# Rotary embedding on one core: VectorE at 8 positions a time, and an early 1 MB store between the second and the third load

## The chip, the cores and the metric

The kernel runs on one core of a Trainium2 chip. The metric is device time in microseconds (us) of that core, lower is better. The profile covers a slightly shorter span than the timed execution (316.0 us against 317.6 us for the kernel before). All positions in time below are counted from the start of the profile's span.

## The reference

The input x is float32, (batch 8, sequence 2048, heads 16, head size 64), 67.1 MB. Neighbouring elements of a head form pairs, and every pair is rotated by an angle that depends on the position. The output has the shape and type of x.

```python
x_pairs = x.reshape(batch, seq_len, num_heads, head_dim // 2, 2)
x1, x2 = x_pairs[..., 0], x_pairs[..., 1]
out1 = x1 * cos - x2 * sin
out2 = x1 * sin + x2 * cos
out = np.stack([out1, out2], axis=-1).reshape(batch, seq_len, num_heads, head_dim)
```

There is little arithmetic for each byte. 67.1 MB must be read and 67.1 MB written.

## The kernel before

One batch is one tile of 128 partitions x 16 positions x 1024 elements. GpSimd's DMA queue loads it and casts it from float32 to bf16 on the way (8 MB are read, 4 MB land in SBUF: 67.63 MB read from HBM in all, and 4096 KB listed for a load), and its stores cast back (67.11 MB written). Five tiles are in flight. Loads and stores are numbered by batch, from 0, so load 2 is the third load. VectorE rotates a tile in place, a few positions at a time, with three instructions: the product with the sine table, the product with the cosine table, and a sum that swaps the neighbours.

```python
KP = 4        # positions in one group of VectorE instructions
NX = 5        # tiles in flight
HEAD = 2      # positions of batch 0 that take another way in
TAIL = 4      # positions of batch 7 that take another way out

def load(b, k0=0):
    if b not in tiles:
        tiles[b] = xpool.tile([P, K, HD], bf16, name="xt")
    nc.gpsimd.dma_start(out=tiles[b][:, k0:], in_=x_t[b, :, k0:])

def store(b, k1=K):
    nc.gpsimd.dma_start(out=out_t[b, :, :k1], in_=tiles[b][:, :k1])

def rotate(b, k0, k1):
    # ... views cut ...
    nc.vector.tensor_tensor(out=rows(qt[:, :nk]), in0=rows(xp), in1=tab(s_tab), op=mult)
    nc.vector.tensor_tensor(out=rows(xp), in0=rows(xp), in1=tab(c_tab), op=mult)
    # ...
    nc.vector.tensor_tensor(out=x3, in0=x3, in1=q_swap, op=add)
```

SyncE's DMA queue brings the first two positions of batch 0 in float32 ("head", 2 x 512 KB), then the cosine table and the sine table (256 KB each). Beside it, GpSimd issues all five loads.

```python
head = stage.tile([P, TAIL, HD], fp32, name="st")
for k in range(HEAD):
    nc.sync.dma_start(out=head[:, k : k + 1], in_=x_t[0, :, k : k + 1])
nc.sync.dma_start(out=cos_sb, in_=cos_t)
nc.sync.dma_start(out=sin_sb, in_=sin_t)
load(0, HEAD)
for b in range(1, NX):
    load(b)

nc.scalar.copy(out=tiles[0][:, :HEAD], in_=head[:, :HEAD])
# ... VectorE makes the bf16 tables s_tab and c_tab from sin_sb and cos_sb ...
for b in range(B):
    if b == 0:
        rotate(b, 0, HEAD)
        rotate(b, HEAD, KP)
    for k0 in range(KP if b == 0 else 0, K, KP):
        rotate(b, k0, k0 + KP)
    if b < B - 1:
        store(b)
    if b >= 1 and b - 1 + NX < B:
        load(b - 1 + NX)
# ... the last batch: 12 positions by GpSimd's queue, 4 by ScalarE's cast and SyncE's queue ...
```

## Time and profile before

The time before is 317.61 us (median of 5 runs, 317.44 to 317.65).

| what | kernel before |
|---|---|
| span of the profile | 316.0 us |
| VectorE busy | 221.8 us, 102 instructions |
| GpSimd's DMA queue, share of 16 engines | 96.8% |
| HBM traffic over the span | 134.7 MB, 426 GB/s |
| sine table lands | 44.2 us |
| last store issued by GpSimd | 262.7 us |

First the page's own lines. The row "DMA" gives the busy share of the DMA engines in 40 equal slices, in tenths, and the q lines give packets, megabytes and share of 16 engines:

```profile
span 316.0 us, 198 instructions
...
DVE 221.8 (70%) x102; ACT 6.9 (2%) x4; POOL 8.9 (3%) x20
...
DMA  9899999999999999999999999999999999999996
...
q0 software_dynamic: 2304, 98.04, 96.8%
q1 hardware_dynamic: 720, 3.67, 3.1%
...
HBM read 67.63 MB, written 67.11 MB: 426 GB/s over the span
```

The DMA engines are full from the second slice to the last but one. VectorE is busy 70% of the span, and nearly all of its idle time lies at the two ends. The reading is that the kernel is bound by its DMA queue.

The packet counts are worth a division. GpSimd's queue made 16 transfers and has 2304 packets, SyncE's made 5 and has 720. Both give 144 packets a transfer, or 9 on each of 16 engines, whether a transfer moves 8 MB or 256 KB. The packed trace also holds the start, length and size of every single packet, which no printed view shows. By these records 8 of the 9 carry data and one carries 4 bytes, and a data packet of load 1 lands 32 KB where one of a table lands 2 KB.

The waits (engine, line, what it waited for: total us, number of times, longest):

```profile
ACT xt L116 <- DMA out_dram<-xt: 286.3, 1, 286.3
POOL out_dram L59 <- DVE xt L80: 202.1, 8, 70.5
POOL xt L56 <- DMA out_dram<-xt: 51.3, 3, 21.7
DVE s_tab L94 <- DMA sin_sb<-in_sin_dram: 44.2, 1, 44.2
```

VectorE's only wait for a DMA is the first one: 44.2 us for the sine table (L94 makes the bf16 sine table). Cosine is already there at 24.04 us (issued at 1.64, 22.4 us to landing). The timeline shows what follows (start, duration, engine, line; L56 is the load, L59 the store, L74, L75 and L80 the three rotation instructions, L116 the copy that waits until the store of batch 6 has landed):

```profile
1.24 2.80 POOL L56 DMA_DIRECT2D xt<-in_x_dram  x5 [0.80 <-PEq L144]
...
44.22 0.45 DVE L94 CAST s_tab<-sin_sb 128x512 bf16<-128x512 f32 x1 [44.22 <-DMA sin_sb<-in_sin_dram]
...
45.50 1.22 DVE L74 TENSOR_TENSOR qt<-xt,s_tab 128x2048 bf16<-128x2048 bf16 x1
...
48.02 1.23 DVE L80 TENSOR_TENSOR xt<-xt,qt 128x2048 bf16<-128x2048 bf16 x1
...
74.53 0.54 POOL L59 DMA_DIRECT2D out_dram<-xt  x1 [70.48 <-DVE xt L80]
...
262.71 0.53 POOL L59 DMA_DIRECT2D out_dram<-xt  x1 [20.41 <-DVE xt L80]
...
295.87 0.19 ACT L116 COPY xt<-xt 1x1 bf16<-1x1 bf16 x1 [286.31 <-DMA out_dram<-xt]
```

All five loads are issued within 4 us. The first store is issued at 74.5 us, the last at 262.7, and the DMA engines are busy until 314.8 us.

### The profile page before, as it was taken

The page shows a single profiled execution, that of the slowest core. Times are in us where ns is not written, and L with a number is a line of the kernel's source. Part 1 is how long each engine was busy: PE and PEld are TensorE (multiplying, and loading weights), DVE is VectorE, ACT ScalarE, POOL GpSimd, SP SyncE. Part 2 cuts the span into 40 slices and gives each one's busy share as a digit, 9 for nine tenths or more (in the row PEclk, how much of TensorE's full clock was granted, in tenths as well). Part 3 has the DMA queues.
Part 4 walks back from the last instruction along what each step waited for, and adds up shares of the span by engine and source line. Part 5 has one row for each costly group of instructions (what it writes and reads, how often), then busy time and mean ns, then how long its engine had stood idle before and what let it go on. Part 6 is the DMA issues. An engine that isn't in the chain of part 4 may idle for free.

```text
span 316.0 us, 198 instructions
## 1 busy us (share of the span) xinstructions
DVE 221.8 (70%) x102; ACT 6.9 (2%) x4; POOL 8.9 (3%) x20
## 2 busy tenths in 40 slices
DVE  0000039999999999999999999999999999100000
ACT  1200000000000000000000000000000000000400
POOL 3000000000000000000000000000000000000000
DMA  9899999999999999999999999999999999999996
GB/s 241 198 257 212 212 207 236 228 199 199 253 212 265 398 498 431 398 332 261 203 399 465 328 203 199 481 448 265 199 307 423 398 440 481 406 398 481 417 431 263
DMA packets 3025, 101.72 MB, mean 322 GB/s; under 512 B 336, under 2 KB 336, under 8 KB 848
## 3 DMA queue, kind: packets, MB, share of 16 engines
q0 software_dynamic: 2304, 98.04, 96.8%
q1 hardware_dynamic: 720, 3.67, 3.1%
q14 instruction: 1, 0.01, 0.0%
HBM read 67.63 MB, written 67.11 MB: 426 GB/s over the span
## 4 chain that ended last, share of the span: by engine, by line
another core or an unknown queue 91%; DMA 2%; ACTq 1%; ACT 1%; SPq 0%; issue 0%
DMA st<-in_x_dram 2%; ACTq L144 1%; ACT xt L92 1%; ACT L92 0%; SPq L85 0%; ACT xt L116 0%; ACTq L116 0%; ACTq L92 0%
## 5 line engine op out<-in xcount | busy, mean ns | idle before, releaser
L75 DVE TENSOR_TENSOR xt<-xt,c_tab 128x4096 bf16<-128x4096 bf16 (+1 forms) x33 | 73.5, 2228 | 1.1
L80 DVE TENSOR_TENSOR xt<-xt,qt 128x4096 bf16<-128x4096 bf16 (+1 forms) x33 | 73.5, 2228 | 1.1
L74 DVE TENSOR_TENSOR qt<-xt,s_tab 128x4096 bf16<-128x4096 bf16 (+1 forms) x33 | 73.5, 2228 | 1.1
L94 DVE CAST s_tab<-sin_sb 128x512 bf16<-128x512 f32 x1 | 0.5, 453 | 44.2 <-DMA sin_sb<-in_sin_dram 44.2
L59 POOL DMA_DIRECT2D out_dram<-xt x8 | 4.3, 535 | 202.1 <-DVE xt L80 202.1
L116 ACT COPY xt<-xt 1x1 bf16<-1x1 bf16 x1 | 0.2, 193 | 286.3 <-DMA out_dram<-xt 286.3
L56 POOL DMA_DIRECT2D xt<-in_x_dram x8 | 4.4, 561 | 52.1 <-DMA out_dram<-xt 51.3
L117 ACT CAST st<-xt 128x4096 f32<-128x4096 bf16 x1 | 3.6, 3599 | 0.0
L92 ACT CAST xt<-st 128x2048 bf16<-128x2048 f32 x1 | 1.9, 1899 | 0.0
L92 ACT ACT_TABLE_LOAD x1 | 1.3, 1283 | 6.4 <-DMA st<-in_x_dram 6.4
L96 DVE CAST c_tab<-cos_sb 128x1024 bf16<-128x1024 f32 x1 | 0.7, 684 | 0.0
L95 DVE TENSOR_SCALAR s_tab<-sin_sb 128x512 bf16<-128x512 f32 x1 | 0.4, 443 | 0.0
L133 POOL MEMSET const-float32-0.0<- 128x1 f32 x1 | 0.1, 99 | 0.2 <-issue 0.2
L133 POOL MEMSET const-bfloat16-1.0<- 128x1 bf16 x1 | 0.1, 102 | 0.0
L133 POOL MEMSET const-float32-1.0<- 128x1 f32 x1 | 0.1, 99 | 0.0
L133 POOL MEMSET const-uint8-127<- 128x1 uint8 x1 | 0.1, 99 | 0.0
## 6 DMA issues: line engine op xcount, KB each, us to landing
xt<-in_x_dram POOLq DMA_DIRECT2D x7, 4096.0 KB, 58.0
out_dram<-xt POOLq DMA_DIRECT2D x1, 6144.0 KB, 49.4
xt<-in_x_dram POOLq DMA_DIRECT2D x1, 3584.0 KB, 22.7
out_dram<-st SPq DMA_DIRECT2D x1, 2048.0 KB, 15.5
st<-in_x_dram SPq DMA_DIRECT2D x2, 512.0 KB, 4.5
cos_sb<-in_cos_dram SPq DMA_DIRECT2D x1, 256.0 KB, 22.4
sin_sb<-in_sin_dram SPq DMA_DIRECT2D x1, 256.0 KB, 42.1
out_dram<-xt POOLq DMA_DIRECT2D x7, 54.0
```

Source lines behind the costliest of these rows:

```text
L56: nc.gpsimd.dma_start(out=tiles[b][:, k0:], in_=x_t[b, :, k0:])
L59: nc.gpsimd.dma_start(out=out_t[b, :, :k1], in_=tiles[b][:, :k1])
L74: nc.vector.tensor_tensor(out=rows(qt[:, :nk]), in0=rows(xp), in1=tab(s_tab), op=mult)
L75: nc.vector.tensor_tensor(out=rows(xp), in0=rows(xp), in1=tab(c_tab), op=mult)
L80: nc.vector.tensor_tensor(out=x3, in0=x3, in1=q_swap, op=add)
L92: nc.scalar.copy(out=tiles[0][:, :HEAD], in_=head[:, :HEAD])
L94: nc.vector.tensor_copy(out=s2[:, :, 0], in_=sin_sb)
L95: nc.vector.tensor_scalar_mul(s2[:, :, 1], sin_sb, -1.0)
L96: nc.vector.tensor_copy(out=c_tab.rearrange("p k (i j) -> p (k i) j", j=2), in_=cos_sb.to_broadcast([P, K * D2, 2]),)
L117: nc.scalar.copy(out=tail, in_=tiles[B - 1][:, K - TAIL :])
L133: nc = _bacc.Bacc("TRN2", target_bir_lowering=False, num_devices=1)
L144: with _tile.TileContext(nc) as tc:
```

## The change

It does two things. VectorE works on 8 positions at a time, so 48 instructions (102 before, 54 after) and their fixed costs go (about 159 ns each, an estimate from 1226 ns at 128x2048 and 2293 ns at 128x4096). And GpSimd, having issued two loads, stores the first two rotated positions of batch 0 (1 MB of output) before it issues loads 2 to 4: output should start to flow early. No byte is added.

```diff
-    KP = 4
+    KP = 8
...
-    def store(b, k1=K):
-        nc.gpsimd.dma_start(out=out_t[b, :, :k1], in_=tiles[b][:, :k1])
+    def store(b, k0=0, k1=K):
+        nc.gpsimd.dma_start(out=out_t[b, :, k0:k1], in_=tiles[b][:, k0:k1])
...
         load(0, HEAD)
-        for b in range(1, NX):
-            load(b)
+        load(1)
...
             if b == 0:
                 rotate(b, 0, HEAD)
+                store(b, 0, HEAD)
+                for c in range(2, NX):
+                    load(c)
                 rotate(b, HEAD, KP)
...
-                store(b)
+                store(b, HEAD if b == 0 else 0)
```

More of the change, by code (lines that the diff above doesn't have):

```diff
@@ L106 @@
             if b < B - 1:
-                store(b)
+                store(b, HEAD if b == 0 else 0)
             if b >= 1 and b - 1 + NX < B:
                 load(b - 1 + NX)
-        store(B - 1, K - TAIL)
+        store(B - 1, 0, K - TAIL)
         tail = stage.tile([P, TAIL, HD], fp32, name="st")
```

## The prediction

> **What bounds the kernel now.** The DMA engines. The slices of the page show them 90% busy or more from the second slice to the last but one, and the queue table gives 96.8% to the GpSimd queue and 3.1% to the SyncE queue. HBM moves 134.7 MB in a 316.0 us span (426 GB/s). VectorE is busy 221.8 us (70%) and in the timeline runs without a gap from 44.2 to 269.4 us, yet the last store issue is at 262.7 and the queue drains until about 314.
>
> **VectorE at 8 positions.** Groups by form: 1226 ns at 128x2048, 2293 ns at 128x4096, so about 159 ns is fixed per instruction (estimate) and one of 128x8192 should take about 4427 ns. 50 instructions fewer save about 9 us of VectorE (busy about 213 us). None of it is on the critical path.
>
> **The early store.** No byte is added or removed. But GpSimd issues in order, and the third load now stands behind a store that waits for the first rotation. That rotation needs the sine table. Its 256 KB, issued at 2.1 us, lands only at 44.2 us. Cosine landed at 24.04 us, and load 0 at about 23.9 (1.24 + 22.7). The DMA engines seem to alternate between the two queues packet by packet[...]. Both queues show 144 packets per full transfer (2304/16 and 720/5), so one small table keeps pace with one 8 MB load, and sine lands when load 1 lands. Estimate from bytes: 23.9 + 8.65 MB/425 GB/s = 44.2 us.
>
> In the old kernel load 2 is already queued then. In the new one the queue is empty at about 44 us, and refilling takes the chain:
> - tables, 44.22 to 45.50: 1.3 us
> - first rotation, three 128x2048: 45.50 to 49.25: 3.75 us
> - VectorE to GpSimd, 0.55 us (as before the first old store), and issue, 0.54 us
> - restart and landing latency, [...] here the first 512 KB load took 3.9 us to land, which leaves about 2.7 us (estimate)
>
> Sum: about 8.2 to 8.8 us with idle DMA engines, between about 43 and 51 us. All of it is critical, because everything after it is a queue that is never empty: loads 2 to 4 and the stores follow back to back and merely move about 8 us later. VectorE would wait for loads 6 and 7 (landing about 209 and 248 us, it being ready about 207 and 236), still ahead of the queue, so harmless.
>
> **Predicted:** 317.6 + 8.4 = 326.0 us; 8 in 10: 322.8 to 328.2. Faster by over 2%: 0.02; within 2%: 0.16; slower by over 2%: 0.82.
>
> **What would show it.** In the new profile: DMA near 0 from about 43.5 to 51 us, the rest unchanged at 1.0; sine still landing near 44 us; GpSimd's first store issue near 49.8; VectorE x52, 128x8192 near 4.43 us, its work no longer gapless near the last batch; store 6 landing, which releases the last copy, near 304 instead of 295.8.
>
> **What would make it wrong.** If sine lands well before load 1, the hole shrinks by as much, toward "same". If stores and loads mixed differently run faster than 430 GB/s, part is won back. If the restart takes longer than 2.7 us, it is slower.

The sum came to 8.2 to 8.8 us. The first terms make 6.1 us; the 2.7 us of the last one is the estimate, and makes the upper end. It comes out as the 3.9 us of the first 512 KB load less its bytes at the measured 426 GB/s (1.2 us).

## More of the kernel before

Last, three windows around the landing of sine (duration, busy time of VectorE, ScalarE and GpSimd with instruction counts, granted clock, DMA share, GB/s):

```profile
core 0: us, DVE busy (x) ACT busy (x) POOL busy (x), PEclk, DMA share, GB/s
40.00:44.00 4.00, 0.00 (x0) 0.00 (x0) 0.00 (x0) 1.00 1.27 279
44.00:50.00 6.00, 5.67 (x7) 0.00 (x0) 0.00 (x0) 1.00 0.81 175
50.00:54.00 4.00, 3.90 (x4) 0.00 (x0) 0.00 (x0) 1.00 1.22 262
```

The queue has no gap here: load 2 was issued long before. This view books a whole packet to the window in which it starts, so a share can exceed 1, and only windows of several us, or an exact 0.00, can be read.

## The result, and the profile after

The changed kernel takes 326.41 us (median of 5 runs, 325.99 to 327.11) against 317.61 us. The ratio is 1.0283, with a 95% interval of 1.0268 to 1.0297: slower. Ratios here and below are not quite the ratios of the quoted medians.

The page of the changed kernel, the lines that answer to those of before:

```profile
span 324.6 us, 153 instructions
...
DVE 214.2 (66%) x54; ACT 6.9 (2%) x4; POOL 9.4 (3%) x21
...
DMA  9899919899899999999899999999999999999996
...
q0 software_dynamic: 2448, 98.04, 94.6%
q1 hardware_dynamic: 720, 3.67, 3.1%
...
HBM read 67.63 MB, written 67.11 MB: 415 GB/s over the span
```

The sixth slice of the DMA row (40.6 to 48.7 us) shows 1 where it showed 9. The queue's share fell from 96.8% to 94.6% with the same bytes, and 144 packets more in GpSimd's queue, those of the extra store. VectorE is 7.6 us less busy, and the span is 8.6 us longer.

The windows of the changed kernel (columns as before):

```profile
40.00:44.00 4.00, 0.01 (x1) 0.00 (x0) 0.00 (x0) 1.00 0.66 147
44.00:50.00 6.00, 5.90 (x7) 0.00 (x0) 0.41 (x1) 1.00 0.00 0
50.00:54.00 4.00, 3.96 (x2) 0.00 (x0) 1.71 (x4) 1.00 1.35 393
```

From 44 to 50 us no packet starts, while VectorE is busy 5.90 of the 6 us. The packet records give the exact size of the hole: the last packet of sine ends at 43.50 us, the next one, the first of the early store, starts at 50.69. For 7.2 us no engine holds a packet. There is no second gap, and the kernel before has none. The timeline shows what they wait for (L93 is the sine table, L119 the copy after the store of batch 6):

```profile
1.25 1.20 POOL L56 DMA_DIRECT2D xt<-in_x_dram  x2 [0.80 <-PEq L147]
...
43.99 0.45 DVE L93 CAST s_tab<-sin_sb 128x512 bf16<-128x512 f32 x1 [43.99 <-DMA sin_sb<-in_sin_dram]
...
45.27 1.22 DVE L74 TENSOR_TENSOR qt<-xt,s_tab 128x2048 bf16<-128x2048 bf16 x1
...
47.78 1.23 DVE L80 TENSOR_TENSOR xt<-xt,qt 128x2048 bf16<-128x2048 bf16 x1
49.05 3.36 DVE L74 TENSOR_TENSOR qt<-xt,s_tab 128x6144 bf16<-128x6144 bf16 x1
49.59 0.54 POOL L59 DMA_DIRECT2D out_dram<-xt  x1 [47.14 <-DVE xt L80]
50.11 1.59 POOL L56 DMA_DIRECT2D xt<-in_x_dram  x3
...
273.37 0.53 POOL L59 DMA_DIRECT2D out_dram<-xt  x1 [38.11 <-DVE xt L80]
304.56 0.19 ACT L119 COPY xt<-xt 1x1 bf16<-1x1 bf16 x1 [295.22 <-DMA out_dram<-xt]
```

The order reads: sine has landed and VectorE starts (43.99 us), tables (to 45.27), the first rotation (to about 49.0), the early store (49.59), and only then the three loads (from 50.11). In the kernel before, those three loads had been issued by 4 us.

The delay is made once and then carried. The copy that waits for the store of batch 6 starts at 295.87 us before and at 304.56 after, 8.7 us later, as the whole span is 8.6 us longer.

VectorE's instructions cost what was expected of them (group by form: count, busy us, mean ns, idle time ahead and its releasers):

```profile
L74 DVE TENSOR_TENSOR qt<-xt,s_tab 128x8192 bf16<-128x8192 bf16 x15 | 66.4, 4425 | 13.7 <-DMA xt<-in_x_dram 13.2
```

VectorE now waits 13.2 us for loads 6 and 7. By the reading of this profile that costs nothing, because the queue ahead of the stores it delays is still full; a run below, which waits 13.7 us for the same loads and takes 317.37 us, shows it.

### The profile page after: what moved, and what is told of

It is laid out like the page before. It is cut to its first block, busy times and chain, and to the rows that moved or that the text cites. A ratio compares the mean times of both kernels' runs of the same rounds, so it can differ in the third digit from the quotient of the medians. Undisturbed runs are those within 1.5% of the kernel's fastest.

```text
span 324.6 us, 153 instructions
## 1 busy us (share of the span) xinstructions
DVE 214.2 (66%) x54; ACT 6.9 (2%) x4; POOL 9.4 (3%) x21
## 3 DMA queue, kind: packets, MB, share of 16 engines
q0 software_dynamic: 2448, 98.04, 94.6%
## 4 chain that ended last, share of the span: by engine, by line
another core or an unknown queue 91%; DMA 2%; ACTq 1%; ACT 1%; SPq 0%; issue 0%
DMA st<-in_x_dram 2%; ACTq L147 1%; ACT xt L91 1%; ACT L91 0%; SPq L85 0%; ACT xt L119 0%; ACTq L119 0%; ACTq L91 0%
## 5 line engine op out<-in xcount | busy, mean ns | idle before, releaser
L74 DVE TENSOR_TENSOR qt<-xt,s_tab 128x8192 bf16<-128x8192 bf16 (+2 forms) x17 | 71.0, 4174 | 13.7 <-DMA xt<-in_x_dram 13.2
L80 DVE TENSOR_TENSOR xt<-xt,qt 128x8192 bf16<-128x8192 bf16 (+2 forms) x17 | 71.0, 4175 | 0.6
L75 DVE TENSOR_TENSOR xt<-xt,c_tab 128x8192 bf16<-128x8192 bf16 (+2 forms) x17 | 71.0, 4175 | 0.6
L93 DVE CAST s_tab<-sin_sb 128x512 bf16<-128x512 f32 x1 | 0.5, 454 | 44.0 <-DMA sin_sb<-in_sin_dram 44.0
L119 ACT COPY xt<-xt 1x1 bf16<-1x1 bf16 x1 | 0.2, 193 | 295.2 <-DMA out_dram<-xt 295.2
L91 ACT CAST xt<-st 128x2048 bf16<-128x2048 f32 x1 | 1.9, 1897 | 0.0
```

The lines of the kernel that those rows point to most:

```text
L93: nc.vector.tensor_copy(out=s2[:, :, 0], in_=sin_sb)
```

## The experiments

The theory is: the DMA queue is the bound. It runs empty when load 1 is done, because load 2 stands in GpSimd's order behind a store that needs the first rotation, which needs sine; and sine lands with load 1, because the DMA engines alternate between the queues packet by packet (in the packet records of the kernel before, sine and load 1 each start a round of packets about every 2.5 us, from 25.2 and from 22.8 us). The rivals are: the longer VectorE instructions cost something; the extra store, or reads mixed with writes, slow the stream; sine takes some 42 us whatever is queued. Ten kernels ran, all with correct results. The kernel before took 317.58 to 317.78 us (medians) beside them.

| run | sine lands, us | early (or first) store issued, us | DMA share, 44 to 50 us | median us | ratio, 95% interval |
|---|---|---|---|---|---|
| before | 44.2 | 74.5 | 0.81 | 317.61 | |
| after | 43.99 | 49.59 | 0.00 | 326.41 | 1.0283 (1.0268 to 1.0297) |
| VectorE part alone | 44.07 | 73.21 | 0.81 | 317.64 | 0.9999 (0.9983 to 1.0016) |
| store part alone | 44.02 | 49.61 | 0.00 | 326.68 | 1.0279 (1.0264 to 1.0294) |
| third load ahead of the store | 44.1 | 49.65 | 0.81 | 317.85 | 1.0005 (0.999 to 1.002) |
| tables first | 4.18 | 51.38 | 0.00 | 329.25 | 1.0365 (1.0327 to 1.0404) |
| after, 3 more products | 44.21 | 53.58 | 0.00 | 330.70 | 1.0411 (1.0393 to 1.0428) |
| before, 3 more products | 44.33 | 78.41 | 0.84 | 317.48 | 0.9997 (0.9982 to 1.0012) |
| load 1 in two halves | 34.53 | 40.12 | 1.09 | 317.37 | 0.9993 (0.9978 to 1.0008) |
| load 1 behind the store too | 24.7 | 30.24 | hole at 24 to 30 | 326.42 | 1.0282 (1.0266 to 1.0297) |
| after, tables on ScalarE's queue | 20.49 | 26.08 | 1.17 | 317.98 | 1.001 (0.9995 to 1.0025) |
| before, tables on ScalarE's queue | 19.98 | 50.42 | 0.91 | 317.79 | 1.0009 (0.9992 to 1.0025) |

### Each part alone

```diff
 # kernel before
-    KP = 4
+    KP = 8
```

> Old kernel with VectorE at 8 positions only. Theory (VectorE is off the critical path, the early store alone costs the time): 317.6 us, ratio 1.000 +- 0.003, VectorE busy 214 us. Rival (the longer VectorE instructions cost time, by later stores or delayed GpSimd issues): over 320 us.

Measured: 317.64 us, ratio 0.9999, VectorE busy 214.2 us. 7.6 us of VectorE time gone change nothing in the total, and the longer instructions do no harm either.

```diff
 # kernel after
-    KP = 8
+    KP = 4
```

> New kernel with VectorE back at 4 positions: the early store alone. Theory: the whole loss, 326.4 us, ratio 1.027 to 1.030, with DMA share 0 from about 44 to 50 us. Rival (the two parts share the loss): 319 to 324 us.

Measured: 326.68 us, ratio 1.0279, DMA share 0.00 from 44 to 50 us. The early store with its place in the order is the whole loss. The rival that the parts share it falls.

### The third load ahead of the store

```diff
 # kernel after
         load(1)
+        load(2)
...
                 store(b, 0, HEAD)
-                for c in range(2, NX):
+                for c in range(3, NX):
                     load(c)
```

> New kernel with the third load issued ahead of the early store; the store remains. Theory (the loss is an empty queue at 44 us): a load of about 20 us covers the rotation, no stretch of DMA share 0, 317.6 us, ratio 1.000 +- 0.003. Rival (the extra store itself, or reads and writes mixed early, slow the DMA engines): stays above 321 us. Sine lands near 44 us in both.

Measured: 317.85 us, ratio 1.0005. The store is issued at the same moment (49.65 us), and sine lands at the same moment, but the engines have load 2 to work on:

```profile
44.00:50.00 6.00, 5.84 (x7) 0.00 (x0) 0.35 (x1) 1.00 0.81 175
```

So neither the extra transfer nor a write among the early reads costs anything that these runs resolve. One issue in front of the wait instead of behind it is worth 8.6 us by the medians.

### The tables first: a miss

```diff
 # kernel after
-        for k in range(HEAD):
-            nc.sync.dma_start(out=head[:, k : k + 1], in_=x_t[0, :, k : k + 1])
         nc.sync.dma_start(out=cos_sb, in_=cos_t)
         nc.sync.dma_start(out=sin_sb, in_=sin_t)
+        for k in range(HEAD):
+            nc.sync.dma_start(out=head[:, k : k + 1], in_=x_t[0, :, k : k + 1])
```

> New kernel with the cosine and sine tables issued ahead of the two head rows, store and third load in the order of the change. Theory (the store is late only because sine is late): sine lands by about 6 us, the first rotation ends near 15 us, the store is issued near 15 us, the queue never empties, 317.6 us, ratio 1.000 +- 0.005. Rival (it is the place of the store in GpSimd's order that costs): stays near 326 us.

Measured: 329.25 us (327.84 to 330.95), ratio 1.0365. The expectation failed: this kernel is even slower than the changed one. The waits show why:

```profile
ACT L91 <- DMA st<-in_x_dram: 43.8, 1, 43.8
DVE qt L74 <- ACT xt L91: 41.5, 1, 41.5
...
DVE s_tab L93 <- DMA sin_sb<-in_sin_dram: 4.2, 1, 4.2
```

Sine landed at 4.2 us as expected, but now the head rows land at 43.8 us (ScalarE's L91 casts them). The expectation had overlooked that two small transfers still stand behind two others in that queue, beside the two loads; only their contents were swapped, and again the last of them landed just before the engines ran dry (DMA share 0.00 from 44 to 50 us). The chain behind the last of them is longer now, because it includes ScalarE's table load and cast (1.28 and 1.90 us): 51.38 - 43.84 = 7.5 us to the store issue, where the changed kernel takes 49.59 - 43.99 = 5.6 us. That explains 1.9 of the 2.8 us between the medians; the rest is not settled, and the runs of this kernel spread over 3 us.

### Three more products, in both kernels

```diff
 # rotate(), in the kernel after and, in another run, in the kernel before
         nc.vector.tensor_tensor(out=rows(qt[:, :nk]), in0=rows(xp), in1=tab(s_tab), op=mult)
+        if b == 0 and k0 == 0:
+            for _ in range(3):
+                nc.vector.tensor_tensor(out=rows(qt[:, :nk]), in0=rows(xp), in1=tab(s_tab), op=mult)
```

> New kernel with the first product of the first rotation computed three more times (same result, 3 x 1.25 = 3.75 us more VectorE ahead of the early store). Theory: the whole chain from sine to the store is critical, so 326.4 + 3.75 = 330.2 us, ratio 1.039 to 1.041. Rival (most of the loss is restart or a slower stream, only part of the VectorE time counts): less than 328.5 us.

> Old kernel with the same three more products ahead of its first rotation. Theory (VectorE has slack, the queue is full): 317.6 us, ratio 1.000 +- 0.003. Rival (VectorE time before the first store counts in the old kernel too): 321.4 us.

Measured: 330.70 us in the changed kernel, 4.3 us more by the medians (ratio 1.0411 against 1.0283), for 3.78 us more VectorE work ahead of the store; 317.48 us in the kernel before, no difference. In the changed kernel the hole grew to the same extent:

```profile
44.00:50.00 6.00, 5.69 (x7) 0.00 (x0) 0.00 (x0) 1.00 0.00 0
50.00:54.00 4.00, 3.90 (x4) 0.00 (x0) 0.42 (x1) 1.00 0.00 0
54.00:58.00 4.00, 3.96 (x2) 0.00 (x0) 1.70 (x4) 1.00 1.39 393
```

The first 3.8 us of a rotation are free in one kernel and cost their full length in the other. By the packet records it now lasts from 43.68 to 54.68 us, 11.0 us instead of 7.2. The 0.5 us beyond 3.78 is of the size of the spread of the runs and is not explained.

### Load 1 in two halves

```diff
 # kernel after
-    def load(b, k0=0):
+    def load(b, k0=0, k1=K):
...
-        nc.gpsimd.dma_start(out=tiles[b][:, k0:], in_=x_t[b, :, k0:])
+        nc.gpsimd.dma_start(out=tiles[b][:, k0:k1], in_=x_t[b, :, k0:k1])
...
-        load(1)
+        load(1, 0, K // 2)
+        load(1, K // 2)
```

> New kernel with the second load issued as two halves of 8 positions, same bytes. Theory (queues alternate packet by packet, 8 data packets per engine and transfer, so the sine table keeps pace with one transfer of whatever size): sine lands near 34 us with the first half, rotation ends near 39 us, the store is issued near 40 us while the second half still runs, no hole, 317.6 us, ratio 1.000 to 1.005. Rival (the two queues share bytes or time, or sine waits for the load to finish): sine stays at 44 us and the time at 326 us.

Measured: sine lands at 34.53 us, the time is 317.37 us, ratio 0.9993. The timeline:

```profile
34.53 0.45 DVE L94 CAST s_tab<-sin_sb 128x512 bf16<-128x512 f32 x1 [34.53 <-DMA sin_sb<-in_sin_dram]
...
40.12 0.54 POOL L59 DMA_DIRECT2D out_dram<-xt  x1 [37.13 <-DVE xt L80]
```

This is the sharpest test of the alternation by a change. The bytes of load 1 are the same, only cut into two transfers (GpSimd's queue has 2592 packets, 144 more than the changed kernel), and sine lands 9.5 us earlier. A share that goes by bytes or by time alone would have left it at 44. One rival passes this test too: that sine simply waits for the one transfer beside it. The packet records of the kernel before rule it out. The data packets of sine do not come in one piece at the end; they start in eight rounds of 16, one for each engine, from 25.2 to 43.6 us, one round about every 2.5 us, as do those of load 1 (2.43 us each). Cosine's come every 2.2 us from 7.3 to 23.5 us, beside those of load 0 (2.13 us each). In the run with the halved load, sine's rounds come every 1.3 us. The store is issued while the second half still runs, so the hole is gone, although the order of load 1, store and loads 2 to 4 is kept. VectorE waits 13.7 us for loads 6 and 7 in this run too, so those waits do no harm.

### Load 1 behind the store too

```diff
 # kernel after
         load(0, HEAD)
-        load(1)
...
-                for c in range(2, NX):
+                for c in range(1, NX):
                     load(c)
```

> New kernel with the second load also behind the early store: only the first load is queued ahead. Theory (once the other queue is empty sine goes through at once): sine lands near 25 us instead of 44, the hole of about 8 us moves to 24 to 32 us and keeps its size, 326 us, ratio 1.025 to 1.031. Rival (sine needs some 42 us whatever is queued): VectorE starts at 44 us, hole of about 27 us, about 345 us.

Measured: sine lands at 24.7 us, the time is 326.42 us, ratio 1.0282. Windows of this run:

```profile
20.00:24.00 4.00, 0.00 (x0) 0.00 (x0) 0.00 (x0) 1.00 0.75 195
24.00:30.00 6.00, 5.24 (x7) 0.00 (x0) 0.00 (x0) 1.00 0.00 1
30.00:34.00 4.00, 3.97 (x2) 0.00 (x0) 2.66 (x5) 1.00 1.38 393
```

The hole moved 19 us forward and cost the same. Sine does not take 42 us of its own. With only load 0 queued it lands at 24.7 us, just after the time at which load 0 landed in the kernel before (23.9 us). With one load in front as with two, the queue is empty at that moment, and the packet records show holes of nearly one size (24.29 to 31.34 us here, 43.50 to 50.69 in the changed kernel). The size of the hole is that of the chain from the table to the next issue, not of anything in the loads.

### The tables on another queue, in both kernels

```diff
 # in the kernel after and, in another run, in the kernel before
-        nc.sync.dma_start(out=cos_sb, in_=cos_t)
-        nc.sync.dma_start(out=sin_sb, in_=sin_t)
+        nc.scalar.dma_start(out=cos_sb, in_=cos_t)
+        nc.scalar.dma_start(out=sin_sb, in_=sin_t)
```

> New kernel with the two table loads issued from ScalarE's queue at the start, beside the head rows on SyncE's, so that neither stands behind the other. The run with the tables first only moved the wait to the head rows (43.8 us), because they then were the last small transfers of that queue. Theory (the order of GpSimd's issues does no harm when the first rotation can start early): tables and head rows all land by 24 us at the latest, the store is issued by 32 us, while load 1 still runs; no hole, 317.6 us, ratio 1.000 +- 0.004. Rival (the place of the store in the order costs by itself): stays above 323 us.

> Old kernel with the same move of the table loads. Theory (VectorE has slack, its earlier start buys nothing as the queue is full anyway): VectorE starts 20 us or more earlier, yet 317.6 us, ratio 1.000 +- 0.003. Rival (the late start of VectorE costs the old kernel something): under 315 us.

Measured: 317.98 us (ratio 1.001) and 317.79 us (ratio 1.0009). In the changed kernel:

```profile
20.49 0.45 DVE L93 CAST s_tab<-sin_sb 128x512 bf16<-128x512 f32 x1 [20.49 <-DMA sin_sb<-in_sin_dram]
...
26.08 0.54 POOL L59 DMA_DIRECT2D out_dram<-xt  x1 [23.63 <-DVE xt L80]
```

With the tables on a queue of their own, sine lands at 20.5 us and the head rows at 16.3. The store is issued at 26.1 us, inside load 1, and the order of the change costs nothing. This is the test that the run with the tables first was meant to be. In the kernel before, VectorE starts 24 us earlier and the time stays: the late start was never a cost there.

No version is faster than the kernel before beyond the noise. Six of the ten variants come within 0.1% of it, with intervals that include 1. Their DMA share from 44 to 50 us is 0.81 to 1.17, and their medians are 317.37 to 317.98 us: no experiment here made the queue drain faster.

## Why the prediction was right

The prediction of 326.0 us (322.8 to 328.2) met 326.41 us. Step by step:

- **The DMA queue bounds the kernel, VectorE does not.** Right. Taking 7.6 us of work from VectorE (ratio 0.9999), adding 3.8 us ahead of its first rotation (0.9997) and starting it 24 us earlier (1.0009) all left the old kernel where it was.
- **The cost of the larger instruction.** Predicted 4427 ns by a line through the two old sizes, measured 4426 ns. The number of instructions was miscounted: 50 fewer and x52 were forecast, 48 fewer and x54 came, so VectorE saved 7.6 us and not about 9. As VectorE is off the critical path, this did not touch the total.
- **Sine lands with load 1.** Right: 43.99 us. The reason given, that the engines alternate packet by packet, was inference from two coinciding times and equal packet counts. The halved load (34.53 us), the missing load (24.7 us) and the exchanged order (head rows at 43.8 us) now test it in three ways, all three agree, and the packet records show the rounds themselves (2.5 us apart beside load 1, 1.3 us beside its half).
- **The length of the hole.** Predicted 8.2 to 8.8 us, the span grew by 8.6. The terms read from the trace: tables 1.28 us, rotation 3.78, hand-over to GpSimd 0.54, issue 0.52. They sum to 6.1 us, and each was forecast within 0.03 us. The term for restart and landing, 2.3 us in the forecast of 8.4 (8.4 less 6.1), was too large: by the packet records 0.5 us pass from sine's last packet (43.50) to VectorE's start (43.99), and 0.6 us from the end of the store's issue (50.11) to its first packet (50.69). With these the chain is 7.2 us, all of the hole, and not the 8.2 to 8.8 us of idle engines that were forecast. The span grew by 1.4 us more than this hole. What fills the 1.4 us was not tested; the 16 engines do run dry one after another (their last packets end between 42.7 and 43.5 us), and the packets of GpSimd's queue took some 1.2 us more in all (96.8% of 316.0 us is 305.9, 94.6% of 324.6 us is 307.1). So the mechanism was right, but that the total came within 0.4 us is in part luck: one term was too large by about what was left out. The 1 MB store landed 4.5 us after its issue, on an empty queue.
- **All of it is critical, later waits are harmless.** Right. VectorE waited 1.3 us for load 6 and 11.9 us for load 7, as forecast (landings near 207.7 and 246.3 us against the predicted 209 and 248), and still the delay of 8.7 us at the store of batch 6 is that of the start.
- **Where it could have failed.** The prediction named an earlier sine table as the way to be wrong. The halved load shows that this was the right place: with sine at 34.5 us the same order of issues costs nothing.

## What to carry to other kernels

When a kernel is bound by one in-order queue, an issue that waits for computed data must not stand in front of the last issues that keep the queue full: check at the moment of the wait how much queued work is left, and compare it with the chain that ends the wait (here no queued work against a chain of 7.2 us). Small transfers beside large ones were served one packet for one packet here, so the first table landed with the first large load (cosine at 24.04 us, load 0 at 23.9) and the second table with the second (sine at 44.2 us; the last packet of load 1 ended at 43.6); look at landing times, not at sizes, before relying on "it is only 256 KB". And when an engine that is not the bottleneck becomes faster, expect nothing (here 7.6 us less VectorE work gave a ratio of 0.9999), but test it alone, so that a gain or a loss of the other half is not put down to it.

## What the packets and queues showed here

- A 256 KB table took as long as the large load beside it (cosine 22.4 us, load 0 22.7 us from issue to landing in the kernel before), and the next table landed with the next load (sine 42.1 us from issue to landing). Cutting one load in two brought sine from 44 to 34.5 us.
- What the trace counts as a packet is large on GpSimd's queue: 98.04 MB in 2304 packets, of which 2048 carry data, about 47.9 KB each. Every transfer took 144 packets, whether 8 MB or 256 KB, and the tables' packets (2 KB) took turns with packets of 28 and 32 KB (as landed in SBUF).
- The same two table loads, moved from SyncE's queue to ScalarE's, brought sine from 43.99 to 20.49 us in the changed kernel, while the time of the kernel before stayed (317.79 against 317.58 us). The issue time saved (sine is issued at 1.17 instead of 2.11 us) is no likely cause: in the kernel before, cosine was issued at 1.64 us, yet by the packet records its first data packet started only at 7.3, behind the head rows' last at 5.8.
